# Pacing the DMA jobs that add up weight blocks, and the place of the last sixteen transposes, in a one-core hybrid layer

## The chip, the core and the metric

The kernel runs on one core of a Trainium2 chip. Five engines matter here: TensorE (PE, with its weight loads as PEld), VectorE (DVE), ScalarE (ACT), GpSimd (POOL) and SyncE (SP), of which SP does nothing but issue DMA transfers. Each engine works through its own list of instructions in order; semaphores make one list wait for another. The metric is the device time of one execution in microseconds (us), as the median of several runs. The profile is one execution, recorded instruction by instruction.

## The reference

One layer on 512 tokens of width 1024, all in float32:

```python
xn = rmsnorm(x, n_mix_pre)
proj = xn @ w_in                                   # 1024 x 14352
qa, ka, va, za, beta_logit, a_dt, qb, kb, vb, gb, gate_a, gate_b = _split_cols(proj, IN_SIZES)
...
oa = chunk_gated_delta_rule(qa, ka, va, beta, g)   # 8 heads, after a causal convolution and silu
oa = rmsnorm(oa, norm_a) * jax.nn.silu(za.reshape(b, s, A_HEADS, A_DV))
ya = oa.reshape(b, s, A_V) @ w_br_a
...
ob = chunk_retention(qb, kb, vb)                   # 4 heads, after a rotary embedding
ob = rmsnorm(ob, norm_b.reshape(B_HEADS, B_DV)) * jax.nn.silu(gb.reshape(b, s, B_HEADS, B_DV))
yb = ob.reshape(b, s, B_V) @ w_br_b
mix = (jax.nn.sigmoid(gate_a) * ya + jax.nn.sigmoid(gate_b) * yb) @ w_out
x = x + rmsnorm(mix, n_mix_post)
hn = rmsnorm(x, n_mlp_pre)
ff = jnp.square(jax.nn.relu(hn @ w_up)) @ w_down
return x + rmsnorm(ff, n_mlp_post)
```

## The kernel before

**Products.** Each float32 product is made of three matmuls on a rounded high part and a low remainder of both factors (mm3, L91). A block of weights, 128 x 1024 values or 512 KB, is loaded by SP into a tile named raw; ACT casts it to the high part whi (L151), and DVE subtracts to get the low part wlo (L152). Both sit in rings of three buffers; raw has two, and two more in the retention stage (tag ych) and the MLP.

**Seven products for eight.** Many weight blocks of 1024 x 1024 are cut into four quarters, and a scheme of seven products replaces the eight of the plain way (seven, L274, named "11", "s1", "s2", "12", "s3", "s4", "22"). It needs sums of weight quarters. These are made by DMA alone: a copy of two k-tiles, 512 KB, from one place of DRAM to another (copy_block, on SP's queue, L173), and later an accumulating DMA that adds another quarter onto it (add_block, on GpSimd's queue, L138, kept in program order on that queue). One copy or one add is a "job". There are 70 of each, in two lists, trickle (copies) and later_adds (adds), in the order in which the sums are used: z, ga, then vg0 to vg3 and br0 to br2 by turns, gb, and dn0 to dn3 for w_down. When a sum is first read, BlockSums.ready forces out whatever jobs of it are left.

**Pacing.** Each load of weights calls pace (L115). It reads a clock, spent[0], that the program keeps while it is written down: each matmul adds its own length to it (tick; in the delta stage the planner's clock.now). If enough of that clock has gone by since the last jobs, a pair of jobs is put out, under issue_after(before[0].ins): what goes to SP's queue is queued behind the load before this one. No jobs run while the clock is under 70 or within REST (860 to 985). The clock isn't the time of the trace; it reads 458 at retention's first load of QB, 584 at the second head's and 1020 at the second MLP group's first load of w_up, which the trace issues at about 430, 575 and 1061.

**Stages.** First a planner (Clock) writes out the order of the delta rule's chunk recurrences with projections as fillers, down to the z gates (late_gates_filler) and the product with w_br_a; all its matmuls are kept in program order. Then come four heads of retention. In each, scores (L1560) computes Q and K (feature_major, four loads of w_in), with the previous head's branch product between; values gives V and its gate by seven; outputs (L1724) ends in scaling the rows o by rstd on ACT (L1744). After the last head, features(3, rows) turns its rows into feature-major form: 16 transposes on PE in four groups of four, each group into the one PSUM bank of tag tr, emptied by ACT (L393) and DVE (L394) into og. Then gate_unit runs the seven products of gate b, the product of og with w_br_b follows, then w_out, and the MLP in four groups: w_up, squared relu, and seven_down with w_down, whose own adds on GpSimd stand on L208.

**Order.** Within a list, instructions are placed by a scheduler at build time, by priority and readiness, unless the program binds them. token_product, which makes the matmuls of a seven, binds every matmul but its first (L332 to L334):

```python
if pinned:
    tc.keep_in_program_order(m)
pinned.append(m)
```

keep_in_program_order puts m behind the instruction written just before it for the same engine. issue_after(ins) puts behind ins only what is written for the engine of ins.

## Time and profile before

| | us |
|---|---|
| median of 3 runs | 1338.36 (1337.3 to 1339.6) |
| the profiled execution's own time | 1340.98 |
| its span, first to last instruction | 1339.1 |
| mean granted TensorE clock | 0.996 |
| ACT, casts to whi from raw (L151), 230 times | 241.7 |
| DVE, wlo from raw (L152), 230 times | 281.0 |

How to read it: the page gives the busy time of each engine, DMA queues and the chain of work that ended last, followed back from the last instruction. In lines by group, the number after "idle before" is how long the engine stood still just before, and the arrow names what ended that. "DMA raw<-in_w_up_dram" is a transfer from the tensor w_up to the tile raw. A busy share near 10 tenths on PE throughout means that the time can be shorter only where PE has holes, or where its clock was reduced:

```profile
PE   9999999999899999999999999999999999999997
PEclk9999999999999999999999999999999999999999
DMA  5437995567787757995795876864548896956335
raw<-in_w_in_dram SPq DMA_DIRECT2D x95, 512.0 KB, 5.3
raw<-in_w_up_dram SPq DMA_DIRECT2D x36, 512.0 KB, 8.2
```

The first three rows are tenths in 40 equal slices of the span; the last two give transfers by kind, with their count, size and the median us from issue to landing.

### The profile page before, as it was taken

How to read it: one execution, taken by the hardware profiler on the slowest of the kernel's cores; microseconds unless marked ns; L12 is line 12 of the kernel's file. 1: busy time of each engine (PE TensorE's matmuls, PEld its weight loads, DVE VectorE, ACT ScalarE, POOL GpSimd, SP SyncE). 2: the span in 40 equal slices, each digit the busy share in tenths (PEclk: the TensorE clock that was granted, in tenths of full speed). 3: DMA queues.
4: the chain of work that ended last, by engine and by line, in shares of the span. 5: the costliest groups of instructions: out<-in, count | busy, mean ns of one | idle time of the engine just before them, and what ended most of it. 6: DMA issues, size and time to landing. Idle time of an engine off the chain costs nothing.

```text
span 1339.1 us, 17596 instructions
## 1 busy us (share of the span) xinstructions
PE 1309.1 (98%) x6555; PEld 1080.5 (81%) x6555; DVE 927.3 (69%) x1554; ACT 698.7 (52%) x1216; POOL 115.2 (9%) x119
## 2 busy tenths in 40 slices
PE   9999999999899999999999999999999999999997
PEld 7888787888688878878878888878888877888886
DVE  6789757486557567768669869768585726738478
ACT  5784546455424425555555554565356627345364
POOL 2101110000011000010010000000000210200001
PEclk9999999999999999999999999999999999999999
DMA  5437995567787757995795876864548896956335
GB/s 180 142 104 184 201 210 121 126 161 187 184 208 204 158 160 196 294 246 134 206 241 146 234 202 187 221 209 153 189 139 236 188 281 178 235 130 139 112 116 136
DMA packets 124149, 243.60 MB, mean 182 GB/s; under 512 B 7638, under 2 KB 39552, under 8 KB 123808
## 3 DMA queue, kind: packets, MB, share of 16 engines
q1 hardware_dynamic: 99808, 183.00, 43.0%
q0 software_dynamic: 21936, 53.12, 23.9%
q10 hardware_dynamic: 2320, 6.36, 1.3%
q8 instruction: 51, 0.84, 0.2%
q14 instruction: 34, 0.28, 0.1%
HBM read 237.20 MB, written 78.66 MB: 236 GB/s over the span
## 4 chain that ended last, share of the span: by engine, by line
PE 75%; DMA 10%; DVE 8%; ACT 5%; issue 1%; ACTq 0%; DVEq 0%; SPq 0%
PE mm L679 15%; PE mm L328 14%; PE dl L328 12%; PE mm L95 7%; PE mm L96 7%; PE mm L97 7%; PE dl L679 5%; DMA raw<-in_w_up_dram 4%; DMA raw<-in_w_in_dram 3%; DVE wlo L152 2%; ACT whi L151 2%; PE tr L408 1%; DMA raw<-sums 1%; PE dl L95 1%; PE dl L96 1%
## 5 line engine op out<-in xcount | busy, mean ns | idle before, releaser
L152 DVE TENSOR_TENSOR wlo<-raw,whi 128x1024 fp32r<-128x1024 f32 x230 | 281.0, 1223 | 203.5 <-ACT whi L151 196.0
L151 ACT CAST whi<-raw 128x1024 fp32r<-128x1024 f32 x230 | 241.7, 1052 | 286.9 <-PE mm L679 62.2
L679 PE MATMUL mm<-actT,whi 128*128 128x512 f32 x448 | 144.5, 404 | 0.0
L95 PE MATMUL mm<-hn,whi 128*128 128x512 f32 (+1 forms) x288 | 106.3, 369 | 5.4 <-ACT r L1945 5.4
L97 PE MATMUL mm<-hn,wlo 128*128 128x512 f32 (+1 forms) x288 | 105.9, 368 | 0.0
L96 PE MATMUL mm<-hn,whi 128*128 128x512 f32 (+1 forms) x288 | 105.8, 367 | 0.0
L679 PEld LDWEIGHTS mm<-actT,whi 128*128 128x128 f32 x448 | 80.6, 188 | 14.8
L679 PE MATMUL mm<-actT,wlo 128*128 128x512 f32 x224 | 87.7, 392 | 0.0
L152 DVE TENSOR_TENSOR wlo<-sum,whi 128x1024 fp32r<-128x1024 f32 x48 | 58.7, 1223 | 25.5 <-ACT whi L151 25.5
L151 ACT CAST whi<-sum 128x1024 fp32r<-128x1024 f32 x48 | 50.6, 1054 | 44.5 <-PE mm L328 22.9
L328 PE MATMUL dl<-whi,ffq 128*128 128x512 f32 x224 | 71.3, 389 | 0.0
L95 PEld LDWEIGHTS mm<-hn,whi 128*128 128x128 f32 x288 | 54.7, 190 | 14.8 <-ACT r L1945 6.1
L679 PE MATMUL mm<-whi,og 128*128 128x512 f32 x192 | 62.3, 397 | 0.0
L96 PEld LDWEIGHTS mm<-hn,whi 128*128 128x128 f32 x288 | 54.7, 190 | 8.8
L97 PEld LDWEIGHTS mm<-hn,wlo 128*128 128x128 f32 x288 | 54.6, 190 | 9.0
L138 POOL DMA_DIRECT2D sums<-in_w_in_dram x28 | 32.4, 1174 | 337.8 <-DMA sums<-in_w_in_dram 315.7
L328 PE MATMUL dl<-whi,xsum 128*128 128x512 f32 x192 | 61.3, 390 | 0.0
L328 PE MATMUL mm<-whi,xsum 128*128 128x512 f32 x192 | 61.3, 390 | 0.0
L679 PE MATMUL mm<-whi,actT 128*128 128x512 f32 x176 | 60.3, 404 | 1.0 <-DVE qf L913 1.0
L328 PE MATMUL mm<-whi,ffq 128*128 128x512 f32 x192 | 60.9, 389 | 0.0
L328 PE MATMUL dl<-whi,actT 128*128 128x512 f32 x192 | 60.9, 389 | 0.0
L1950 DVE TENSOR_TENSOR ffq<-r,ffq 128x512 fp32r<-128x512 f32 (+1 forms) x64 | 39.2, 622 | 27.4 <-ACT ffq L1950 27.2
(426 smaller groups left out, 3043.3 us busy)
## 6 DMA issues: line engine op xcount, KB each, us to landing
raw<-in_w_in_dram SPq DMA_DIRECT2D x95, 512.0 KB, 5.3
raw<-sums SPq DMA_DIRECT2D x58, 512.0 KB, 4.7
sums<-in_w_in_dram SPq DMA_DIRECT2D x44, 512.0 KB, 6.7
raw<-in_w_up_dram SPq DMA_DIRECT2D x36, 512.0 KB, 8.2
sums<-in_w_in_dram POOLq DMA_DIRECT2D x28, 512.0 KB, 7.9
sums<-sums POOLq DMA_DIRECT2D x26, 512.0 KB, 8.5
raw<-in_w_down_dram SPq DMA_DIRECT2D x18, 512.0 KB, 3.9
raw<-in_w_br_a_dram SPq DMA_DIRECT2D x16, 512.0 KB, 5.3
```

The costliest lines, as they stand in the source:

```text
L95: nc.tensor.matmul(ps, lh, rh, start=first, stop=False)
L96: nc.tensor.matmul(ps, lh, rl, start=False, stop=False)
L97: triples.append(nc.tensor.matmul(ps, ll, rh, start=False, stop=last))
L138: tc.keep_in_program_order(nc.gpsimd.dma_start(dst, src, accum_op=ALU.add))
L151: nc.scalar.copy(hi[:, :n], raw[:, :n])
L152: nc.vector.tensor_tensor(lo[:, :n], raw[:, :n], hi[:, :n], ALU.subtract)
L328: m = nc.tensor.matmul(pss[t], lhs[i // 2], rhs[i % 2], start=first and k + i == 0, stop=k + i == kts + 1, skip_group_check=not first,)
L408: nc.tensor.transpose(ps, src, ident)
L679: m = tc.keep_in_program_order(nc.tensor.matmul(*args, **kwargs))
L1950: return nc.scalar.copy(dst[0], r), nc.vector.tensor_tensor(dst[1], r, dst[0], ALU.subtract)
```

## The change

In pace, the stretch of the clock from 455 to 860 (DENSE, the retention stage) keeps pairs of jobs, with smaller numbers: 5.8 for a pair in place of 6.6, and 1.7 for a load in place of 2.0. Outside it, in the delta stage and the MLP, each call of pace puts out at most one job, a copy or an add by which list is longer, at intervals of at least 7.5 (delta stage) or 9.6 (MLP) on the clock; loads no longer count there, and the job is put under issue_after of the load that calls, not of the one before it. At the end of retention, the transposes and emptyings of features(3) and the two tiles of gates are written only when gate_unit's second product, s1, has been written; a new yield in seven marks that point, and triples, a list of last matmuls, now takes in token_product's too, so that the transposes can be put behind the last one of s1.

```diff
-JOBS_FROM, JOB_US, LOAD_US = 70.0, 6.6, 2.0
+JOBS_FROM, JOB_US, PAIR_US, LOAD_US = 70.0, (7.5, 9.6), 5.8, 1.7
-REST = 860.0, 985.0
+REST, DENSE = (860.0, 985.0), (455.0, 860.0)
...
         if now < JOBS_FROM or REST[0] < now < REST[1]:
             queued[0] = now
-        elif before[0] is not None:
-            queued[0] = max(queued[0], now - 2.5 * JOB_US)
+        elif now < DENSE[0] or now > DENSE[1]:
+            if queued[0] < now and (trickle or later_adds):
+                queued[0] = max(queued[0] + JOB_US[now > DENSE[1]], now - 8.0)
+                with tc.issue_after(load.ins):
+                    if len(later_adds) > len(trickle):
+                        add_block()
+                    else:
+                        copy_block()
+        else:
+            queued[0] = max(queued[0], now - 2.5 * PAIR_US)
             with tc.issue_after(before[0].ins):
-                while queued[0] + JOB_US < now and (trickle or later_adds):
+                while queued[0] + PAIR_US < now and (trickle or later_adds):
                     if trickle:
                         copy_block()
                     if len(later_adds) > len(trickle) + 1 or not trickle:
                         add_block()
-                    queued[0] += JOB_US
+                    queued[0] += PAIR_US
             queued[0] += LOAD_US
...
         times(c, "s1", raws(sums.raw, 1), True)
         v1 = copied(c, "v1")
+        yield
...
                             start=first and k + i == 0, stop=k + i == kts + 1, skip_group_check=not first,
                         )
+                        triples.append(m)
...
-            for _ in seven(sums, token_product(quarters), tmp, out, lambda: spare(tag)):
-                pass
+            for i, _ in enumerate(seven(sums, token_product(quarters), tmp, out, lambda: spare(tag))):
+                if i and between:
+                    between()
...
-        og = features(3, rows)
-        ya, gates = [], []
+        ya, gates, og = [], [], []
...
-            gates.append(pb_.tile([P, 2, D], F32, tag=("qr", "kr")[i], name="tb"))
...
-        gate_unit(gb_sums, gate_b, "s")
+        def last_features():
+            with tc.issue_after(triples[-1].ins):
+                og.extend(features(3, rows))
+            gates.extend(pb_.tile([P, 2, D], F32, tag=tag, name="tb") for tag in ("qr", "kr"))
+
+        gate_unit(gb_sums, gate_b, "s", last_features)
```

## The prediction

> **What bounds the kernel now.** I read first the page's head, then the PE rows of the waits, then the chain of work that ended last, and the windows around the holes that these show.

> ```profile
> span 1339.1 us, 17596 instructions
> PE 1309.1 (98%) x6555; PEld 1080.5 (81%) x6555; DVE 927.3 (69%) x1554; ACT 698.7 (52%) x1216; POOL 115.2 (9%) x119
> PE mm L95 <- ACT r L1945: 5.4, 2, 5.0
> PE dl L679 <- ACT vt L1362: 2.6, 1, 2.6
> PE dl L95 <- ACT vr L1708: 2.4, 2, 1.8
> PE dl L679 <- ACT vt L1381: 2.2, 1, 2.2
> PE tr L408 <- ACT o L1744: 0.9, 1, 0.9
> 340.00:360.00 20.00, 16.32 (x72) 13.04 (x70) 8.34 (x12) 6.65 (x13) 0.81 (x1) 1.00 0.78 194
> 360.00:380.00 20.00, 18.83 (x76) 15.37 (x77) 10.26 (x15) 11.12 (x25) 3.44 (x3) 0.91 0.78 195
> 1080.00:1100.00 20.00, 20.00 (x90) 16.57 (x89) 3.67 (x3) 5.04 (x6) 4.44 (x4) 1.00 1.07 283
> 1100.00:1120.00 20.00, 14.95 (x60) 11.99 (x59) 7.22 (x10) 11.84 (x21) 0.87 (x1) 0.91 0.91 264
> ```

> TensorE is the bound: 1309.1 of 1339.1 us. No product gets shorter, so all that can move is the 30.0 us of holes, of which the five rows (us in total, times, longest) hold 13.5. A window row gives busy time and count of PE, PEld, DVE, ACT, POOL, then granted clock, DMA share and GB/s. After two holes the clock reads 0.91 for 20 us: 0.09 x 20 = 1.8 us more lost at each.

> ```profile
> 313.67 3.54 DMA raw<-in_w_in_dram
> 319.63 6.38 DMA raw<-sums
> 328.44 5.63 DMA raw<-sums
> 339.01 7.87 DMA raw<-in_w_in_dram
> 350.68 8.94 DMA raw<-in_w_br_a_dram
> 580.16 16.08 DMA raw<-in_w_in_dram
> 674.93 14.95 DMA raw<-in_w_in_dram
> 1063.03 19.08 DMA raw<-in_w_up_dram
> 1084.53 20.27 DMA raw<-in_w_up_dram
> ```

> These pieces of the chain (start, us) stand before those holes: a weight load of 512 KB that takes 3.54 us in a quiet moment takes 8 to 20. ACT runs in order, so the cast (L151) that waits for a late load holds back the ACT instruction behind it that PE needs.

> **Price of a job.**

> ```profile
> q1 hardware_dynamic: 99808, 183.00, 43.0%
> q0 software_dynamic: 21936, 53.12, 23.9%
> 580.71 1.14 POOL L138 DMA_DIRECT2D sums<-in_w_br_b_dram  x1 [29.26 <-DMA sums<-in_w_br_b_dram]
> ```

> A job moves 0.524 MB. q1 (loads and copies) spent 0.430 x 1339.1 = 576 us on 183.00 MB: 1.65 us of all 16 engines for a copy or a load. q0 (adds) spent 320 us on 53.12 MB: 3.16 us for an add. The last row shows when an add starts: GpSimd had idled 29.26 us for its copy. So it is the copies, on SP's queue, that are paced, and each add follows its own copy. "Single jobs at even intervals" thus means a copy every 2 x 7.5 = 15 us in the delta stage and every 19.2 us in the MLP, with its add right behind it. The change doesn't alter the clock that pacing reads, so each load keeps its time. Working both rules through the loads gives, as copies + adds: delta stage 31 + 30 before, 21 + 20 after; retention 30 + 30, then 39 + 39; MLP 9 + 10, then 10 + 11. All 140 jobs remain; the change moves traffic from the delta stage to retention and stretches it in the MLP.

> **Part 1, MLP.**

> ```profile
> sums<-in_w_down_dram SPq DMA_DIRECT2D x5, 512.0 KB, 18.8
> sums<-in_w_down_dram POOLq DMA_DIRECT2D x5, 512.0 KB, 15.2
> sums<-sums POOLq DMA_DIRECT2D x1, 512.0 KB, 10.5
> 1053.76 5.17 POOL L138 DMA_DIRECT2D sums<-in_w_down_dram  x4
> 1104.90 1.04 ACT L151 CAST whi<-raw 128x1024 fp32r<-128x1024 f32 x1 [4.87 <-DMA raw<-in_w_up_dram]
> ```

> The first three rows are the DMA view of 1047 to 1101: 5 copies and 6 adds beside w_up's loads, with four adds issued at once at 1053.76, since they stood on GpSimd's queue behind L208's adds. By the new rule 3 copies and 4 adds fall here, and only one or two at the burst. That frees 2 x 1.65 + 2 x 3.16 = 9.6 us of engine time at a DMA share of 1.07, and the load that ends the hole is 4.87 us late. I take the whole hole and its slow clock: 5.0 + 1.8 = **-6.8 us**; bounds -6.8 and 0. The copies removed here come at 1104 to 1217, where no PE hole stands now; casts run ahead of PE there and hide them. Without that cover, two delayed loads would cost about 2 us.

> **Part 2, delta stage.** Around 297 to 361 the rate hardly falls (old rule: 6.6 us a pair plus 2.0 us a load, with a load each 3.5 us). What changes is place: a copy now goes behind the load that calls for it, not ahead of it. Ahead of the load issued at 339.01 one copy goes; before that of 350.68 a copy and an add go (1.65 + 3.16 = 4.8). Needed are 2.2 and 2.6 us. The first is met only if the chain also gains at 319.63, which had a copy just before it in the queue. Of 2.2 + 2.6 + 1.8 = 6.6 us I take **-5**; bounds -6.6 and 0. What comes late next is the recurrence itself, which the same planner has in time elsewhere. From 160 to 210 three copies replace seven, but the small holes there wait for DVE work, so I count nothing.

> [...]

> **Part 3, retention's denser pairs.**

> ```profile
> 596.34 1.04 ACT L151 CAST whi<-raw 128x1024 fp32r<-128x1024 f32 x1 [2.97 <-DMA raw<-in_w_in_dram]
> 597.92 0.73 PE L95 MATMUL dl<-vr,s 128*128 128x512 f32 x2 [1.78 <-ACT vr L1708]
> 781.84 1.05 ACT L151 CAST whi<-raw 128x1024 fp32r<-128x1024 f32 x1 [0.91 <-DMA raw<-in_w_in_dram]
> ```

> At the head changes (about 580, 675, 768) each load of QB and KB already comes last. The third of these four loads has three copies ahead of it in SP's queue under either rule (two pairs at the first load; the third moves from the third load to the second), so in queue order it loses nothing. But a pair is added before the first head change, its copy near 556 and its add near 571 to 578, just when the three copies run; at the third its add runs near 758 to 765. An add beside a load takes about half the engines' time for some 6 us, so 3 us. At the first place PE already waits 1.78 us, so most counts: +2.5. At the third the cast is 0.91 us late and PE hides it, so +0.8; at the second the added pair is done in time, 0. Together **+3.3**; bounds -2.4 (both holes of L1708 go) and +12 (about 4 us a place).

> [...]

> **Part 4, last transposes.**

> ```profile
> 888.33 0.39 PE L328 MATMUL mm<-wlo,xsum 128*128 128x512 f32 x1
> 889.66 0.33 PE L408 MATMUL tr<-cmat,o 128*128 128x128 f32 x1 [0.94 <-ACT o L1744]
> 898.06 0.60 PE L408 MATMUL tr<-cmat,o 128*128 128x128 f32 x4
> 898.69 0.69 ACT L393 ACTIVATE og<-tr,vecs 128x512 fp32r<-128x512 f32 x1 [0.53 <-PE tr L408]
> 899.41 0.75 DVE L394 SCALAR_TENSOR_TENSOR og<-tr,vecs,og 128x512 fp32r<-128x512 f32 x1 [0.89 <-ACT og L393]
> 900.35 0.60 PE L408 MATMUL tr<-cmat,o 128*128 128x128 f32 x4
> 902.90 0.33 PE L408 MATMUL tr<-cmat,o 128*128 128x128 f32 x1
> ```

> Now the 16 transposes float between the gate's matmuls, and PE waits 0.94 us for the scaled rows before the first. Behind s1 those rows are ready or nearly so, and this goes. But the next product, s2, can't hide them: token_product pins each matmul behind the PE instruction written before it (L332, L333), and s2's first is then written behind the sixteenth transpose. The groups of four share one PSUM bank (tag tr), which ACT and DVE must empty between groups. The rows give 900.35 - 898.06 = 2.29 us from group to group, and 902.90 - 900.35 = 2.55 where a wlo split came between; mean 2.42, of which PE works 0.60. Today matmuls fill the rest; pinned, nothing does: 3 x 1.8 = 5.5 us, less 0.94, plus about 0.5 for the copies of c ahead of the first emptying: **+5.0**. Bounds: -0.9 (all hidden) and +8 (each turnover behind one more 1.2 us split). The loads of ya on ACT's queue and the tiles of gates lose no time, since their first use lies behind s1. The extra yield and the longer list of triples issue nothing.

> **Sum.** -6.8 - 5.0 + 3.3 + 5.0 = -3.5 us. The profiled execution took 1340.98 us (span 1339.1 and 1.9 around it), which becomes 1337.5. It lay 2.6 us above the median of the three runs, 1338.36, so the forecast is **1334.9**.

> **Rivals.**
> - *Transposes hidden.* If s2's matmuls do mix with them, part 4 is -0.9 and the sum -9.4: 1329. Against it stands the pin in the code; for it, that unpinned transposes mix freely now.
> - *Slower: retention's pairs crowd out QB's and KB's loads.* At the three head changes part 3 becomes +12 once a load lands over 1 us later than now, as its casts have no lead left (0.91 and 2.97 us late). Sum +5.2: 1343.5. For it: nine pairs more in this stage; against it: the queue order of the third load.
> - *The delta stage's load chain is bound by its two raw buffers*, not by jobs: each load waits for the wlo split of the one two before. Part 2 is then 0, the sum +1.5: 1340. Its quiet 3.54 us and its later 6 to 9 speak against it.
> - *The jobs aren't spread.* GpSimd's adds pile up behind L208's as at 1053.76, and the MLP hole stays: sum +3.3, 1341.7.

> **How the numbers follow.** Forecast 0.42, transposes hidden 0.17, slower pairs 0.20, buffers 0.13, not spread 0.08. About 0.2%, 2.7 us, is what a measurement of this kernel tells from no change. Faster takes 0.26 of the forecast's 0.42 (it lies just past that bound), the 0.17 and a little of the buffers' case: 0.45. Slower takes most of the pairs' case, half of the last and the forecast's upper tail: 0.25. Within 0.2%: 0.30. For 8 in 10 the range runs from the hidden transposes to the slower pairs, 1328.5 to 1343.5; the forecast's own, by the bounds of parts 2 to 4, is 1331 to 1339.

> **What would show it.** Right: no PE wait for r (L1945) near 1101 and a clock of 1.00 there; none for vt (L1381, L1362) at 346 to 361; sixteen transposes in a row between s1 and s2, with three waits for og (L394) of about 1.8 us; longer waits for vr (L1708) near 595. Wrong: transposes among s2's matmuls, holes of over 3 us near 690 or 780, or the hole near 1101 still there, with the jobs moved.

## The result, and the profile after

| | before, us | after, us |
|---|---|---|
| median of 7 runs each, on the same chip | 1337.3 (1334.91 to 1340.75) | 1332.15 (1328.77 to 1334.92) |
| the profiled execution's own time | 1340.98 | 1328.77 |
| its span | 1339.1 | 1327.0 |

The ratio after to before is 0.9956, with a 95% interval from 0.9938 to 0.9974. The forecast was 1334.9. The two profiled executions aren't in the middle of their runs: before's is longer than any of its seven, after's the shortest of its seven. Their spans differ by 12.1 us where the medians differ by 5.15. So each kernel was profiled a second time, and both pairs are used below. On another chip (e4 below) the kernel after took 1331.93 us against 1334.65, a ratio of 0.9979 with an interval from 0.9956 to 1.0002, so the gain is clear on the first chip alone.

First, of the page after, the head and the rows of TensorE's busy share and clock, and the waits of TensorE (engine, tile and line that waited, then the releaser; us in total, times, longest), then windows over the same stretches as before.

```profile
span 1327.0 us, 17591 instructions
PE   9999999999999999999999999989999999999997
PEclk9999999999999999999999999989999999999999
```

```profile
PE tr L418 <- DVE og L404: 6.1, 3, 3.0
```

```profile
340.00:360.00 20.00, 20.00 (x91) 16.87 (x90) 13.94 (x21) 13.42 (x27) 1.14 (x1) 1.00 0.82 219
...
1100.00:1120.00 20.00, 20.00 (x90) 16.57 (x89) 11.94 (x15) 12.96 (x20) 1.77 (x2) 1.00 0.52 125
```

The waits for r and for both vt are gone, TensorE is busy through both windows (the one from 360 and the one from 1080 read the same, 20.00 and 1.00), and the clock stands at 1.00 in them. In their place is one new wait, three times for og, 6.1 us. It is the slice of 8 tenths on the PE row, and the clock's only one. The timeline there (start, us, engine, line; in brackets the idle time before it and its releaser):

```profile
879.49 0.81 PE L418 MATMUL tr<-cmat,o 128*128 128x128 f32 x4
883.31 0.66 PE L418 MATMUL tr<-cmat,o 128*128 128x128 f32 x4 [3.01 <-DVE og L404]
885.53 1.12 PE L418 MATMUL tr<-cmat,o 128*128 128x128 f32 x4 [1.56 <-DVE og L404]
888.21 1.12 PE L418 MATMUL tr<-cmat,o 128*128 128x128 f32 x4 [1.56 <-DVE og L404]
888.98 0.78 PE L337 MATMUL dl<-whi,xsum 128*128 128x512 f32 x1
```

All sixteen transposes run before s2's first matmul, as the pin says, and between groups TensorE does nothing.

**By stages.** Every trace of this study has 6555 instructions on TensorE. The table takes the time between the starts of the same-numbered instruction (1658, 2453, 4439, 4592, 5394 and 5646, which before's first profile starts at 250, 430, 870, 905, 1061 and 1125 us), and gives what each profile needs beyond that of e3, the quickest kernel below. Instructions that float can cross a boundary, so a few tenths mean nothing. The column to 250 isn't the edits' doing: it stands out for the two profiles in which TensorE runs only 35 matmuls in the first 12 us (before's first and e7), where the other twelve have 46 to 48.

| us beyond e3 | to 250 | delta, 250 to 430 | retention, 430 to 870 | gate b, 870 to 905 | to 1061 | MLP, 1061 to 1125 |
|---|---|---|---|---|---|---|
| before, first profile | 1.7 | 7.3 | 2.3 | 0.7 | 0.5 | 6.8 |
| before, second (e8) | 0.4 | 7.0 | 1.8 | -0.2 | -0.1 | 4.3 |
| after, first profile | 0.0 | 0.0 | -0.6 | 7.8 | -0.1 | 0.0 |
| after, second (e4) | -0.1 | 0.0 | 2.5 | 9.1 | -0.1 | 0.0 |
| e1 | -0.1 | 1.4 | 1.3 | 0.1 | -0.1 | 0.0 |
| e2 | 0.0 | 4.1 | 2.0 | 11.3 | -0.1 | 6.2 |
| e5 | 0.0 | 5.4 | 2.4 | 3.5 | -0.1 | 0.0 |
| e6 | 0.0 | 0.9 | 2.5 | -0.8 | -0.1 | 4.6 |
| e7 | 1.9 | 0.0 | 5.4 | 3.6 | 0.1 | 0.0 |
| e9 | 0.0 | 6.9 | 0.7 | 0.9 | 0.0 | 0.0 |
| e10 | -0.1 | 1.5 | 2.4 | 5.5 | -0.1 | 0.0 |
| e11 (e3 again) | 0.0 | 0.0 | 1.6 | -0.6 | 0.0 | 0.0 |
| e12 | 0.0 | 0.0 | 1.4 | 4.9 | -0.1 | 0.0 |

The change gains some 7 us in the delta stage and 4 to 7 in the MLP, and gives back 7 to 9 at the moved transposes.

### The profile page after: what moved, and what is told of

It reads as the page before. It is cut to its first block, busy times and chain, and to the rows that moved or that the text cites. A ratio compares the mean times of both kernels' runs of the same rounds, so it can differ in the third digit from the quotient of the medians.

```text
span 1327.0 us, 17591 instructions
## 1 busy us (share of the span) xinstructions
PE 1304.4 (98%) x6555; PEld 1080.2 (81%) x6555; DVE 927.9 (70%) x1554; ACT 699.2 (53%) x1216; POOL 115.1 (9%) x119
## 3 DMA queue, kind: packets, MB, share of 16 engines
q1 hardware_dynamic: 99808, 183.00, 42.8%
q0 software_dynamic: 21936, 53.12, 23.5%
## 4 chain that ended last, share of the span: by engine, by line
PE 84%; DVE 8%; ACT 5%; DMA 2%; issue 1%; ACTq 0%; DVEq 0%
PE mm L689 17%; PE mm L337 15%; PE dl L337 14%; PE mm L96 8%; PE mm L95 8%; PE mm L97 8%; PE dl L689 5%; DVE wlo L160 2%; PE tr L418 1%; PE dl L96 1%; PE dl L95 1%; PE dl L97 1%; PE tr L698 1%; DMA raw<-in_w_in_dram 1%; ACT whi L159 1%
## 5 line engine op out<-in xcount | busy, mean ns | idle before, releaser
L95 PE MATMUL mm<-hn,whi 128*128 128x512 f32 (+1 forms) x288 | 105.3, 366 | 0.0
L95 PEld LDWEIGHTS mm<-hn,whi 128*128 128x128 f32 x288 | 54.3, 189 | 8.8
## 6 DMA issues: line engine op xcount, KB each, us to landing
raw<-in_w_in_dram SPq DMA_DIRECT2D x95, 512.0 KB, 5.2
raw<-sums SPq DMA_DIRECT2D x58, 512.0 KB, 4.2
sums<-in_w_in_dram SPq DMA_DIRECT2D x44, 512.0 KB, 6.3
raw<-in_w_up_dram SPq DMA_DIRECT2D x36, 512.0 KB, 6.6
sums<-in_w_in_dram POOLq DMA_DIRECT2D x28, 512.0 KB, 7.9
sums<-sums POOLq DMA_DIRECT2D x26, 512.0 KB, 7.3
raw<-in_w_down_dram SPq DMA_DIRECT2D x18, 512.0 KB, 4.8
raw<-in_w_br_a_dram SPq DMA_DIRECT2D x16, 512.0 KB, 4.4
```

Of the source, the lines that this page charges most:

```text
L95: nc.tensor.matmul(ps, lh, rh, start=first, stop=False)
```

## The experiments

Times are medians; "before" is the kernel before on the same chip beside them, 1334.65 us for e1 to e4, 1336.96 for e5 to e8, 1335.05 for e9 to e11, 1335.81 for e12. Line numbers shift a little with each edit.

### The transposes: e1 to e4 and e12

**e1**, the change without its last part:

```diff
-        ya, gates, og = [], [], []
+        og = features(3, rows)
+        ya, gates = [], []
...
+            gates.append(pb_.tile([P, 2, D], F32, tag=("qr", "kr")[i], name="tb"))
...
-        gate_unit(gb_sums, gate_b, "s", last_features)
+        gate_unit(gb_sums, gate_b, "s")
```

> The changed kernel with its last transposes written ahead of gate b again; pacing as changed. Theory (transposes in a row between s1 and s2 cost PE three waits for the emptying of one PSUM bank, plus a slow clock behind them): the three waits for og of 6.1 us in all go, a wait of about 1 us for o before the first transpose comes back, and the time falls by 5 to 6.5 us against the changed kernel, to about 1326. Rival (the waits are paid elsewhere, since the gate's products then wait for weights): within 1.5 us of the changed kernel.

**e2**, the reverse: the kernel before, with its old pacing, and the last part of the change alone:

```diff
-        og = features(3, rows)
-        ya, gates = [], []
+        ya, gates, og = [], [], []
...
-        gate_unit(gb_sums, gate_b, "s")
+        gate_unit(gb_sums, gate_b, "s", last_features)
```

> The kernel before with the last transposes moved behind s1, and its old pacing. Theory: slower than before by 5 to 6.5 us, three waits for og of 1.5 to 3 us each. Rival (the move is worth something, the pacing is not): faster than before by about 1 us.

**e3**, the whole change, but s2's first matmul isn't bound behind the transposes:

```diff
-                        if pinned:
+                        if loose:
+                            loose.pop()
+                        elif pinned:
                             tc.keep_in_program_order(m)
...
                 og.extend(features(3, rows))
+            loose.append(True)
             gates.extend(pb_.tile([P, 2, D], F32, tag=tag, name="tb") for tag in ("qr", "kr"))
```

> The changed kernel, with the one matmul that is written right behind the sixteen transposes (the first of s2) no longer bound behind them. Theory (the binding makes the three waits): the transposes mix with s2's matmuls again, the waits for og fall under 1 us in all, and the time falls by 6 to 7.5 us against the changed kernel, below the kernel with the transposes ahead by about 1 us. Rival (s2 could not have started, for lack of weights or banks): the same waits and the same time as the changed kernel.

**e4** is the kernel after, unchanged, on the chip of these three.

> The changed kernel once more, for a second profile: its first profiled execution was the fastest of its seven, that of before the slowest of its seven, and the spans differ by 12.1 us where the medians differ by 5.2. If the holes near 346, 358 and 1101 are gone in every execution, the second profile shows them gone too; if they come and go, one of them is back. Time 1329 to 1335.

Measured: e1 1323.15 us (ratio to before 0.9921, 0.9894 to 0.9949), e2 1344.64 (1.0075, 1.0052 to 1.0099), e3 1322.42 (0.9914, 0.9887 to 0.9942), e4 1331.93 (0.9979, 0.9956 to 1.0002). The last part alone costs 10.0 us on top of the old pacing and 8.8 on top of the new one (e4 less e1). Taking one binding away gives back 9.5. All three went the way that was expected and further: 5 to 6.5 us had been set for e1 and e2, 6 to 7.5 for e3. What the move is worth without the binding can't be told from nothing: e3 is 0.7 us quicker than e1, and their ranges overlap. The waits of e2, then of e3:

```profile
PE tr L410 <- DVE og L396: 6.1, 3, 3.0
PE mm L95 <- ACT r L1951: 4.3, 1, 4.3
```

```profile
PE tr L420 <- ACT o L1756: 0.6, 1, 0.6
```

The same 6.1 us for og as after stands in e2; in e3 there is none, and as its timeline shows, groups of transposes stand 2.30 and 3.01 us apart and matmuls of gate b run between them (of s2, then of the next product):

```profile
885.63 0.60 PE L420 MATMUL tr<-cmat,o 128*128 128x128 f32 x4
887.93 0.60 PE L420 MATMUL tr<-cmat,o 128*128 128x128 f32 x4
890.94 0.66 PE L420 MATMUL tr<-cmat,o 128*128 128x128 f32 x4
```

**e12** leaves the pin and gives the transposes a second bank:

```diff
+        other = psx.tile([P, 4, P], F32, tag="dl", name="tr", bufs=3)
         for f in range(4):
-            ps = psx.tile([P, 4, P], F32, tag="tr", name="tr", bufs=1)
+            ps = other if f % 2 else psx.tile([P, 4, P], F32, tag="tr", name="tr", bufs=1)
```

> The kernel after with one edit: the groups of four transposes take turns between the bank of tag tr and a free bank of tag dl; s2's first matmul stays pinned behind the sixteenth transpose, and the order of work is unchanged. Theory (what TensorE waits for in the pinned stretch is the one bank, emptied by ACT and VectorE one group at a time): the third group waits only for the first emptying of VectorE (some 2 us, as that is late behind a split), the fourth hardly, so waits for og fall from 6.1 to about 2 us, the slow clock there goes in part, and the time falls from 1332 to 1325 to 1328 us. Rival (ACT and VectorE are the limit, busy with copies and splits, and a second bank only moves the waits): og 4.5 us or more, 1330 to 1332 us.

Measured: 1327.09 us (0.9935, 0.9915 to 0.9955). Its timeline and window:

```profile
881.41 0.49 PE L418 MATMUL tr<-cmat,o 128*128 128x128 f32 x3
882.07 0.77 PE L418 MATMUL tr<-cmat,o 128*128 128x128 f32 x5 [0.17 <-ACT o L1755]
885.40 1.97 PE L418 MATMUL tr<-cmat,o 128*128 128x128 f32 x8 [2.57 <-DVE og L404]
```

```profile
880.00:900.00 20.00, 17.26 (x72) 14.08 (x72) 10.65 (x12) 10.19 (x15) 0.00 (x0) 0.83 0.37 108
```

Two groups run at once, one wait of 2.57 us is left, and the last two groups follow as one. So it takes both: the pin, which leaves TensorE nothing else to do, and the single bank, which makes it wait for each emptying. The 2.57 us that stay are the first emptying, which is late for a reason of its own; VectorE's timeline in the kernel after:

```profile
881.37 1.23 DVE L160 TENSOR_TENSOR wlo<-raw,whi 128x1024 fp32r<-128x1024 f32 x1 [0.61 <-ACT whi L159]
882.51 0.75 DVE L404 SCALAR_TENSOR_TENSOR og<-tr,vecs,og 128x512 fp32r<-128x512 f32 x1
884.73 0.75 DVE L404 SCALAR_TENSOR_TENSOR og<-tr,vecs,og 128x512 fp32r<-128x512 f32 x1 [1.47 <-ACT og L403]
```

The first group is done at 880.3, but VectorE has a split of weights to finish first.

### The pacing: e5, e6 and e9

These three, and all that follow but e8, are built on e3, whose runs lie close together (1321.48 to 1323.17 us; again, as e11, 1321.04 to 1323.38).

**e5** keeps of the pacing only the MLP's single jobs:

```diff
-JOBS_FROM, JOB_US, PAIR_US, LOAD_US = 70.0, (7.5, 9.6), 5.8, 1.7
+JOBS_FROM, JOB_US, PAIR_US, LOAD_US = 70.0, (7.5, 9.6), 6.6, 2.0
-REST, DENSE = (860.0, 985.0), (455.0, 860.0)
+REST, DENSE = (860.0, 985.0), (0.0, 860.0)
```

> The kernel after with s2's first matmul free of the transposes, and with the old numbers for pairs (6.6 and 2.0) everywhere but in the MLP, which keeps its single jobs. So of the pacing only part 1 is left. Theory: part 1 takes the wait for r (4.3 to 5.4 us) and its slow clock, and parts 2 and 3 are the rest of what the pacing brings: waits for vt (about 2 to 5 us) and vr (about 2 us) come back, the wait for r stays away; 1327 to 1331 us. Rival (all of the pacing's gain lies in the MLP): 1322 to 1324 us, though waits for vt and vr may show. Rival (part 1 brings nothing): over 1332 us.

**e6** keeps all but the MLP's single jobs:

```diff
-        elif now < DENSE[0] or now > DENSE[1]:
+        elif now < DENSE[0]:
...
+            pair, per = (PAIR_US, LOAD_US) if now <= DENSE[1] else (6.6, 2.0)
```

> The same free transposes, new pacing in delta stage and retention, but pairs by the old numbers (6.6 and 2.0) in the MLP. Theory: the wait for r near 1100 (4 to 5 us) and about 2 us of slow clock come back, all else as with free transposes and the new pacing (1322.4 us): 1327 to 1330 us. Rival (a smaller backlog of pairs at the MLP's start, or a hole that comes and goes by chance, is enough to hide it): 1322 to 1324.5 us and a wait for r under 1 us.

Measured: e5 1330.03 us (0.9951, 0.9928 to 0.9973), e6 1329.01 (0.9951, 0.9929 to 0.9974). So the MLP's single jobs are worth 6.6 us (e6 less e3), and delta stage and retention together 7.6 (e5 less e3). The waits of e5, then of e6:

```profile
PE dl L95 <- ACT vr L1720: 2.4, 3, 1.1
PE tr L420 <- ACT o L1756: 2.0, 2, 1.3
PE dl L691 <- ACT vt L1393: 1.9, 1, 1.9
```

```profile
PE mm L95 <- ACT r L1963: 2.9, 1, 2.9
```

Each wait comes back with its own rule: vt in the delta stage in e5, r in the MLP in e6. In e5, 3.5 of the 7.6 us appear at gate b, where the wait for the scaled rows is 2.0 us; e9, with the same rule in retention and the same place of the transposes, shows 0.9 there, so this share may vary from one execution to the next.

**e9** asks what in the delta stage helps: it is e5 with each pair's copy queued behind its own load, 31 copies and 30 adds as before.

```diff
-            with tc.issue_after(before[0].ins):
+            with tc.issue_after((load if now < 455 else before[0]).ins):
```

> As e5_mlp_only (single jobs in the MLP alone, pairs by the old numbers elsewhere, free transposes; 1330.0 us), but in the delta stage each pair's copy is queued behind the load that calls for it instead of the one before. The jobs in the delta stage stay 31 copies and 30 adds; the order on TensorE, ACT, VectorE and GpSimd is the same. Theory (the prediction's: what changes around 297 to 361 is the place of the copy in the queue, not the rate): the waits for vt fall from 2.5 us to under 1, and the stretch of the delta stage that e5 loses against the free transposes with the new pacing (5.3 us of TensorE's time from the 2027th to the 2453rd matmul) shrinks to under 2; 1325 to 1327.5 us. Rival (it is the number of jobs, 31 + 30 against 21 + 20, or that they come as pairs): vt still 2 us or more, 1329 to 1331.5 us.

Measured: 1328.67 us (0.9956, 0.9935 to 0.9977), 1.4 less than e5, with ranges that overlap, and between the times set for the theory and for its rival. Its first row of waits, and from its chain and GpSimd's timeline a load and an add:

```profile
PE dl L691 <- DVE vt L1358: 3.4, 2, 2.5
```

```profile
355.75 9.06 DMA raw<-in_w_br_a_dram
```

```profile
354.30 0.81 POOL L146 DMA_DIRECT2D sums<-sums  x1 [11.46 <-DMA sums<-in_w_br_b_dram]
```

The holes at 346 and 358 are gone, as the theory said, but a new one of 2.5 us stands at 365: an add issued at 354.30 now meets a load of w_br_a, which takes 9.06 us, and the casts and splits behind it are late. The delta stage takes 6.9 us more than in e3, no less than e5's 5.4. The place alone moves the hole. Whether fewer jobs or their single spacing does the rest, no run here separates.

### Retention: e7 and e10

**e7** queues each pair's copy behind the load that calls for it, and leaves the order on TensorE, ACT, VectorE and GpSimd as it is:

```diff
-            with tc.issue_after(before[0].ins):
+            with tc.issue_after(load.ins):
```

> Free transposes and the new pacing, but in retention each pair's copy is queued behind the load that calls for it, not behind the one before it; the numbers and the jobs are the same, and so is the order on TensorE, ACT and VectorE. The third copy at a head change so stands again just ahead of the third of the four loads of QB and KB, where it stood in the kernel before. Theory (what the denser pairs gained there is that this copy came one load earlier): the third load at about 571 us lands in 16 us or more instead of 14.6, waits for vr rise from 0.3 to 2 to 3 us, 1324.5 to 1328 us. [...]

Measured: 1332.79 us (0.9976, 0.9956 to 0.9997), 10.4 more than e3, and more than the theory's 1328 (of the 10.6 us of its profile in the table, 1.9 belong to the start). From the chain and the waits:

```profile
666.80 17.97 DMA raw<-in_w_in_dram
```

```profile
PE dl L95 <- ACT vr L1720: 3.7, 1, 3.7
PE tr L420 <- ACT o L1756: 2.4, 2, 1.6
```

The place of the hole was another than expected: not the first head change but the second, where the third load of QB and KB takes 17.97 us, and gate b, where a copy now goes out at 877.07, between the loads of s2's two held sums (876.68 and 877.73). The traces also show that the edit didn't do what was expected of it at the head changes. Counted in loads on SP's queue, 27 of retention's 39 copies go out one load later than in e3, but the third copy at the first head change doesn't: it is issued between the second and the third load of QB and KB in both, at 568.89 in e3 (the loads at 568.46 and 571.18) and at 572.55 in e7 (571.66 and 574.17). The copy that stands at gate b moved by four loads. That the copies' places count is shown; which one does the harm at the second head change, and whether the denser pairs gain by a copy's place at the first, is not.

**e10** gives retention single jobs too, one every 5.2 on the clock, 38 copies and 39 adds:

```diff
-JOBS_FROM, JOB_US, PAIR_US, LOAD_US = 70.0, (7.5, 9.6), 5.8, 1.7
+JOBS_FROM, JOB_US, PAIR_US, LOAD_US = 70.0, (7.5, 5.2, 9.6), 5.8, 1.7
-        elif now < DENSE[0] or now > DENSE[1]:
+        elif True:
```

> Free transposes and the new pacing, but retention too puts out single jobs, one for a load at most, at intervals of 5.2 on the clock, each behind its own load: 38 copies and 39 adds in retention and 11 + 11 in the MLP, against 39 + 39 and 10 + 11. Theory (at the head changes what counts is that copies are queued ahead of the last loads of QB and KB, however they are grouped): a copy or an add still falls behind each of these loads, vr 1 to 3 us, and the scaled rows at the end wait for late sums as in e7; 1324 to 1329 us. Rival (even spacing is what helps, everywhere): 1320 to 1322.5 us, no wait for vr. Rival (retention's loads leave no room for single jobs): over 1330 us.

Measured: 1332.89 us (0.9996, 0.9974 to 1.0018), 10.2 more than e11 beside it. Its first row of waits, and a row of ACT's timeline:

```profile
PE tr L420 <- ACT o L1756: 4.2, 2, 3.5
```

```profile
880.95 1.05 ACT L159 CAST whi<-sum 128x1024 fp32r<-128x1024 f32 x1 [1.55 <-DMA sum<-sums]
```

Single jobs are no gain in retention. Most of the loss stands at gate b, 5.5 us by the table, and as in e7 a copy goes out between the loads of the two held sums there (873.68, between 873.29 and 874.34): ACT waits for the late sum, with the scaling of the rows behind that cast. That points to the place behind the own load again, but spacing and place change together here: single jobs ahead of the load before weren't tried.

### The second profiles: e8 and e11

> The kernel before once more, for a second profile. Theory (its holes at 346, 358 and 1101 are of its job order): all three are there again, vt 4 to 5 us, r 4 to 5.5 us, vr 2 to 2.5 us, within 1 us of the first profile each. Rival (they come and go between executions, and the first profile, a slow one of its runs, shows more of them than the median has): one or more of them is gone or under half.

e8, the kernel before, took 1334.91 us:

```profile
PE mm L95 <- ACT r L1945: 2.4, 1, 2.4
PE dl L679 <- ACT vt L1381: 2.2, 1, 2.2
PE dl L679 <- ACT vt L1362: 1.9, 1, 1.9
PE dl L95 <- ACT vr L1708: 1.7, 3, 0.9
```

All holes are there again, so they belong to the order of the jobs, but their size isn't fixed, and the theory's "within 1 us" fails for r: the wait for r is 2.4 us here, 2.9 in e6, 4.3 in e2 and 5.4 in the first profile.

> e3_unpin once more, beside the two above on the same chip. Theory: 1321.5 to 1323.5 us, waits for og none, no vt, r under 0.5 us. If it lies over 1325 us, the comparison of runs of different calls that the stages rest on doesn't hold.

e11 took 1322.66 us (0.9918, 0.9887 to 0.995), 0.24 from e3 on another chip, so differences between runs on different chips may be read. It and e3 are the quickest kernels here: the change with one binding less.

## Why the prediction was right, and where its terms were not

The time, 1332.15, lies in the range and in the forecast's own range of 1331 to 1339. That it came so near the forecast is in good part luck. By the runs, parts 1 to 3 brought 11.5 us (e1 less before) where 8.5 were set, and part 4 cost 8.8 to 10.0 where 5.0 were set, so errors of 3 and 4 to 5 us nearly cancel.

| part | predicted, us | by stages, first and second pair of profiles | by runs |
|---|---|---|---|
| 1, MLP | -6.8 | -6.8, -4.3 | e3 less e6: -6.6 |
| 2, delta stage | -5 | -7.3, -7.0 | parts 2 and 3, e3 less e5: -7.6 |
| 3, retention | +3.3 | -2.9, +0.7 | |
| 4, last transposes | +5.0 | +7.1, +9.3 | e4 less e1: +8.8; e2 less before: +10.0 |

**Part 1** was right in mechanism and size: the hole and its slow clock went, no other hole came up, and casts ran ahead of TensorE where the moved jobs landed. Its working took the first profile's hole of 5 us as the kernel's; e8 shows that it varies, which the step had no way to see from one execution, so the close match in size is partly luck.

**Part 2** was right in sign, and low: both holes went whole, and the stage's loss stands at them alone. By the count of the table, before's first profile loses 2.5 us to e3 across the first and 4.7 across the second, and TensorE waits nowhere else from 250 to 430. That is 0.7 more than the bound of -6.6, which added up the two waits and one slow stretch. Its reason, that "what changes is place", was half the story: in e9 the two holes go by place alone, and another comes.

Its reading of the clock, 1.8 us for one hole and nothing for the other, was of one execution; the last section shows what the windows say.

**Part 3** failed. Its reading of the queue holds in effect, as three copies stand ahead of the third load under either rule, though the third copy didn't move (it is between the second and the third load before and after). The step that failed was that the extra pair's "add near 571 to 578" would run just when the three copies do. The chain of the kernel after has the third load of QB and KB there:

```profile
571.22 14.40 DMA raw<-in_w_in_dram
```

14.40 us, against 16.08 before: the extra add wasn't in its way. GpSimd's timeline has its start:

```profile
556.67 0.85 POOL L146 DMA_DIRECT2D sums<-sums  x1 [18.31 <-DMA sums<-in_w_br_b_dram]
```

It was released when its copy landed, and over at 565.8, 5 us before the third load went out (all of it some 9 us earlier than before, by the gains ahead of it). The working had let it start some 5 us later against the loads, though by its own row an add starts as its copy lands. The half of the engines' time that it gave to adds beside a load is near what the traces show: q0, the adds' queue, took 41.7% from 580.2 to 596.3 us in before and 53.1% from 571.2 to 585.6 in after. Over all profiles with the new numbers retention takes -0.6 to 2.5 us beyond e3, with the old ones 0.7 to 2.4 (e7 and e10, which change the place, aside): no difference that these runs can tell, where +3.3 was set. The +0.8 and the 0 for the other head changes have no test of their own.

**Part 4** was right in mechanism, three waits for og of which two measure 1.56, and e3 and e12 confirm both the pin and the bank. It was mis-sized in two places. The first turnover took 3.01 us, not 1.8, behind the split (+1.2); the bounds had named this case, but for all turnovers alike. And the slow clock after a hole, counted in parts 1 and 2, was left out here: the last section's windows give 2 us and more.

**The rivals.** Transposes hidden: this didn't happen, but e3 shows what it would have been, 1322.4, well under the 1329 set for it, as the parts before it gained more. Slower by retention's pairs: not here, though e7 shows that late loads at a head change can cost a good part of the +12 once copies stand later (a wait of 3.7 us for vr, and 5.4 us over retention by the table). Two raw buffers, and jobs not spread: refuted by the holes that went.

## What to carry to other kernels

Before moving work behind a step "where it is ready", look at what the next step is bound to: a binding to the instruction written before it turned sixteen idle-time fillers into 6 us of waiting, and one binding taken away was worth more than the net effect of the whole change. A background transfer did its harm here where it stood just ahead of a load that TensorE waits for (in e9, an add at 354.30 us and then a load of 9.06); queueing retention's copies behind their own loads cost about as much (10.4 us, e7) as the whole new pacing brought (11.5), so look at each such load, and check in the trace which copies an edit really moved. And profile twice before summing holes: one execution's hole of 5 us was 2.4 in the next.

## What the runs showed of the hardware that wasn't expected

```profile
884.00:886.00 2.00, 0.47 (x2) 0.47 (x3) 0.75 (x1) 0.69 (x1) 0.00 (x0) 0.58 0.74 242
886.00:888.00 2.00, 0.65 (x4) 0.25 (x2) 0.59 (x1) 0.69 (x1) 0.00 (x0) 0.50 0.00 1
888.00:890.00 2.00, 1.79 (x7) 1.59 (x8) 0.16 (x1) 0.63 (x1) 0.00 (x0) 0.50 0.00 0
890.00:892.00 2.00, 2.00 (x8) 1.62 (x7) 0.75 (x1) 0.05 (x1) 0.00 (x0) 0.71 0.00 0
```

```profile
1106.00:1108.00 2.00, 1.50 (x4) 1.23 (x5) 1.63 (x2) 1.94 (x4) 0.00 (x0) 0.54 1.06 235
1108.00:1110.00 2.00, 2.00 (x7) 1.61 (x6) 0.43 (x2) 1.97 (x6) 0.00 (x0) 0.61 1.02 202
```

Cut at their edges, as further down, the stretches read 0.50 or 1.00 and nothing between, so a window of 2 us at 0.58 spent 2 x (1 - 0.58) x 2 = 1.68 us at half. Summed, the kernel after spends 1.68 + 2 + 2 + 1.16 = 6.84 us at half, and before, after one hole of 5 us, 1.84 + 1.56 = 3.40: two stretches and one. The cost is about half of what TensorE works meanwhile: in before, 128x512 matmuls start 0.43 us apart at 1108.37 (clock 0.50) and 0.23 at 1109.86 (1.00). In the kernel after it is busy for 0.39 + 0.65 + 1.79 + 1.16 = 4.0 us of the slow stretch (of the first and last window the slow share), so about 2.0 are lost; with the 6.1 of waits and less the 0.6 that e3 waits for o, that makes 7.5, and the stage table has 7.8. The second profile of after (e4) has a slower window:

```profile
880.00:900.00 20.00, 13.74 (x53) 10.62 (x52) 9.14 (x10) 8.56 (x13) 0.00 (x0) 0.74 0.27 82
```

20 x 0.26 x 2 = 10.4 us at half, three stretches after the same 6.1 us of waits, and the table has 9.1 there. In e12 one wait of 2.57 us was followed by 0.83 over 20 us, 6.8 us at half, as long as after's.

The slow stretches of one trace lie on a grid. In before's first profile they begin at 362.06, 1106.16 and 1334.86 us, the second and third 744.10 and 972.80 us after the first, which is 218 and 285 times 3.4133. In after's they begin at 884.36 and 1321.27, 436.91 us apart, 128 times 3.4133. Here are windows cut along that grid, of before, then of e5:

```profile
344.99:348.40 3.41, 1.61 (x8) 0.99 (x6) 0.00 (x0) 1.43 (x3) 0.00 (x0) 1.00 0.87 322
358.65:362.06 3.41, 0.89 (x4) 0.66 (x4) 1.22 (x1) 2.37 (x5) 0.00 (x0) 1.00 0.62 240
362.06:365.47 3.41, 3.41 (x10) 2.57 (x9) 1.78 (x3) 2.34 (x5) 1.17 (x1) 0.50 0.57 159
```

```profile
344.94:348.35 3.41, 1.55 (x8) 1.29 (x8) 1.47 (x2) 3.25 (x8) 0.26 (x1) 1.00 0.37 139
348.35:351.77 3.41, 3.41 (x10) 2.65 (x9) 2.37 (x4) 1.42 (x3) 0.55 (x1) 0.50 0.70 86
```

Before's hole of 2.21 us, from 346.60 to 348.81, is split by the window's edge at 348.40. Its window has 1.61 us of work on TensorE, and no slow stretch follows (the clock reads 1.00 from 340 to 360). The shorter hole of e5, 1.86 us from 345.05 to 346.91, lies within one window, which has 1.55 us of work, and a slow stretch follows. Cut in this way from 20 us on, the traces of before and after have five windows at full clock with up to 1.27 us of work (0.89, 0.00 and 0.00; 0.66 and 1.27), and each is followed by a slow one; of those with 1.61 us or more none is. In e12 one is: the window from 881.01, with 1.65 us of work, 1.25 of it transposes. The 0.91 after before's hole of 2.6 us is the slow stretch behind the window from 358.65, which has 0.89 us of work. So a hole of 1.86 us was followed by a slow stretch and one of 2.21 us wasn't: whether a hole cost some 1.7 us more than its length (half of 3.41) went in these traces with how it fell on the windows, which the prediction didn't ask. Whether its transposes set e12's window apart isn't settled by these runs.

**The job order also sets the spread.** The kernel before ranges from 1325.66 to 1342.95 us over these runs, e3 and e11 from 1321.04 to 1323.38. This fits that where no load is late enough to stop TensorE, what varies in the transfers doesn't reach the end; no run tests it by itself.
